# The running sum of squares of a pre-norm, added by DMA transfers in place of VectorE, in a two-layer encoder trunk

## The chip, the core and the metric

The kernel runs on one core of a Trainium2 chip. The core's engines have queues of their own and work side by side: TensorE (PE in the profile; PEld is its loading of weights), VectorE (DVE), ScalarE (ACT), GpSimd (POOL) and SyncE (SP). SP issues the transfers of the kernel before; 16 DMA engines carry them. The metric is the device time of one execution in microseconds (us), as the median of the runs.

## The reference

A streaming encoder trunk of two layers on 1024 frames of width 1024, in float32. Each layer has a mixer (layer 0: stick-breaking attention beside a multi-scale pooling; layer 1: gated linear attention) and then a gated MLP with a causal depthwise convolution of width 3. Both have an RMS norm ahead. Cut to the part around the change:

```python
def rms_norm(x, gain):
    y = x * rsqrt(mean(x * x, axis=-1) + 1e-6)
    return y * gain

def conv_ffn(h, w_up, conv_w, conv_b, w_down):
    u = h @ w_up                              # 1024 -> 2 * 2816
    conv = conv_b + sum(conv_w[j] * shifted(u, j) for j in range(3))
    a, g = split(conv, 2, axis=-1)
    return (silu(a) * g) @ w_down

for layer in range(2):
    x = x + mixer(rms_norm(x, mix_norm))
    x = x + conv_ffn(rms_norm(x, ffn_norm[layer]), ...)
```

## The kernel before

The residual stream lies transposed in SBUF: eight tiles `x[m]` of 128 partitions (channels) x 1024 (frames). A tile is 512 KB. Every float32 product is made as three matmuls of float32r halves: a value is split into a rounded part `hi` (a cast or a scaled copy by ScalarE) and the remainder `lo` (a subtraction by VectorE), and `hi*hi + hi*lo + lo*hi` is summed in PSUM. `HALVES` are the two halves of 512 frames, `T0` and `T1` in the MLP.

The RMS norm is not applied to `x` ahead of the up-projection. The products are made from `x` times the gain, and what comes out of PSUM is multiplied by `rstd_bc`, the reciprocal root of the mean square, spread over the partitions (`evacuate`, L961). The sum of squares over channels is built in two steps: each tile is squared by ScalarE (L299 for the first tile, straight into `self.acc`; L302 for the other seven, into a tile `sq`) and added to `self.acc`; then `stats` (L254) sums `acc` over the partitions by eight small matmuls with ones. From there ScalarE takes the root (L257), VectorE the reciprocal (L259) and a diagonal (L261), and `spread` (L268, L269) makes `rstd_bc`.

The entry into the up-projection is the stretch of `ffn` from L939 to L955. It goes through the tiles in `ORDER`, (0, 4, 1, 5, 2, 6, 3, 7). For each tile the last part of the mixer's output projection is added (`add_tiles`, L772), `nm.add` stores the tile to DRAM (L288, issued by SP) and makes its blocks and its square, and TensorE fills in with the first two column tiles of the up-projection for the tile two steps earlier (`first_tile`). Then come the last two of these, `nm.stats`, one more column tile (`plain`, with weights split at L796 and L797), `nm.spread`, and the evacuation.

```python
        for n, m in enumerate(ORDER):
            if n >= 2:
                add_tiles(ow, mixt, otags, [m])
            nm.add(m, x[m])
            if n >= 2:
                first_tile(n - 2)
```

`NormBlocks.block` (L282 by ScalarE, L283 by VectorE) makes the split halves of a tile, `blk`. `rsums` (L858 to L861) and `rblock` (`split`, L817 and L818) prepare sums of tiles for the products of the main loop; their tiles are `T1` to `T4`.

TensorE's order is the program's. The other engines' orders are set by a list scheduler that simulates the program while it is built. Tiles come from rotating pools: `self.acc` and the squares take slots of `xpool` (11 slots of one tile), the eight `x[m]` another eight, so there are two slots for squares; whoever takes a slot next waits until its last user is done. In the profile the sum is `nacc`, and a square is `ndg` in layer 0 and `nsq` in layer 1 (names of the slot's tile).

Of the kernel before, what the change touches and what calls it, by code (L numbers as in the profile page):

```python
# [14 lines left out]
ALU = mybir.AluOpType  # L15
# [41 lines left out]
def trunk_kernel(  # L57
# [23 lines left out]
    V, S, G, PE = nc.vector, nc.scalar, nc.gpsimd, nc.tensor  # L81
# [71 lines left out]
    class Filler:  # L153
# [3 lines left out]
        def add(self, *gens):  # L157
            self.gens += gens
# [112 lines left out]
    class NormBlocks(Norm):  # L271
# [14 lines left out]
        def add(self, m, x):  # L286
            xs[m] = dram.tile([P, T], F32, tag=f"xs{self.layer}_{m}", name="xs")
            nc.sync.dma_start(xs[m], x)  # L288
            g = pcol(self.col + m)
            if m < KT // 2:  # L290
                self.b11.append(self.block(x[:, 0:512], g))
                self.b12.append(self.block(x[:, 512:T], g))
            else:
                self.b21.append(self.block(x[:, 0:512], g))
                self.b22.append(self.block(x[:, 512:T], g))
            self.n += 1
            if self.n == 1:
                self.acc = self.acc_tile()
                S.activation(self.acc, x, AF.Square)  # L299
            else:  # L300
                sq = self.sq_tile()
                S.activation(sq, x, AF.Square)  # L302
                V.tensor_tensor(self.acc, self.acc, sq, op=ALU.add)
            if m < KT // 2:
                S.activation(x, x, AF.Copy, scale=g)

# [22 lines left out]
    def pcol(c):  # L329
        return prm[:, c:c + 1]  # L330
# [760 lines left out]
    op = ev.enter_context(tc.tile_pool(name="odd", bufs=1, reuse_waits="tile"))  # L1091
# [324 lines left out]
```

## Time and profile before

| what | before |
|---|---|
| time, median of 3 runs | 2284.07 us (2279.87 to 2284.77) |
| the profiled execution's own time | 2284.64 us |
| its span | 2282.9 us |
| TensorE busy | 2221.5 us, 97% of the span |
| VectorE busy | 1638.4 us, 72% |
| ScalarE busy | 1018.5 us, 45% |
| GpSimd busy | 360.0 us, 16% |
| DMA traffic | 178.54 MB, 78 GB/s on the mean |
| share of TensorE in the chain that ended last | 84% |

All times inside the profile are us from the start of the span. A row of a timeline gives the start, the duration, engine, line, operation, output<-input and shape, and in brackets how long the engine had been idle before it and what ended that. A row of a line gives the least, median and greatest duration in ns and the first and last start. The chain that ended last is followed back from the last instruction to what released each one. "us to landing" of a transfer runs from its issue to the arrival of its data. Layer 0's entry runs from about 430 to 493 us, layer 1's from about 1571 to 1632 us.

### The profile page before, as it was taken

How to read it: one execution, taken by the hardware profiler on the slowest of the kernel's cores; microseconds unless marked ns; L12 is line 12 of the kernel's file. 1: busy time of each engine (PE TensorE's matmuls, PEld its weight loads, DVE VectorE, ACT ScalarE, POOL GpSimd, SP SyncE). 2: the span in 40 equal slices, each digit the busy share in tenths (PEclk: the TensorE clock that was granted, in tenths of full speed). 3: DMA queues.
4: the chain of work that ended last, by engine and by line, in shares of the span. 5: the costliest groups of instructions: out<-in, count | busy, mean ns of one | idle time of the engine just before them, and what ended most of it. 6: DMA issues, size and time to landing. Idle time of an engine off the chain costs nothing.

```text
span 2282.9 us, 27335 instructions
## 1 busy us (share of the span) xinstructions
PE 2221.5 (97%) x10648; PEld 1830.4 (80%) x10648; DVE 1638.4 (72%) x2226; ACT 1018.5 (45%) x1539; POOL 360.0 (16%) x221
## 2 busy tenths in 40 slices
PE   8989989999999999999999999999999999999999
PEld 7878878877888887888887878787778888878887
DVE  5677688799999998554536555557999999985543
ACT  6667766454444444221246262527544444442210
POOL 2351330001111112421110000000011111123210
PEclk9999999999999999999999999999999999999999
DMA  4000121222222226421011011112222222264311
GB/s 143 20 30 29 48 78 53 95 84 81 83 83 83 84 83 209 160 95 53 10 39 45 21 47 38 47 38 92 84 74 83 83 84 83 83 213 147 102 47 74
DMA packets 51427, 178.54 MB, mean 78 GB/s; under 512 B 5968, under 2 KB 6608, under 8 KB 51296
## 3 DMA queue, kind: packets, MB, share of 16 engines
q1 hardware_dynamic: 51296, 176.78, 23.3%
q8 instruction: 84, 1.38, 0.2%
q14 instruction: 47, 0.39, 0.1%
HBM read 140.06 MB, written 36.70 MB: 77 GB/s over the span
## 4 chain that ended last, share of the span: by engine, by line
PE 84%; DVE 5%; ACT 4%; issue 3%; DMA 1%; POOL 1%; SPq 0%; POOLq 0%; DVEq 0%; ACTq 0%
PE lin L838 14%; PE z L838 10%; PE lin L137 6%; PE lin L139 5%; PE lin L141 5%; PE t L838 5%; PE d L838 5%; PE z L137 3%; PE z L139 3%; PE z L141 3%; PE t L137 3%; PE t L139 3%; PE t L141 3%; PE d L137 2%; PE d L139 2%
## 5 line engine op out<-in xcount | busy, mean ns | idle before, releaser
L123 ACT CAST whi<-wraw 128x1024 fp32r<-128x1024 f32 (+4 forms) x108 | 107.7, 999 | 358.2 <-PE d L139 229.8
L1030 POOL TENSOR_TENSOR c<-c 128x1024 f32<-128x1024 f32 x44 | 109.5, 2489 | 900.1 <-ACT c L1029 883.7
L864 DVE TENSOR_TENSOR u<-u,rstd_bc 128x512 f32<-128x512 f32 x160 | 159.4, 998 | 2.6
L124 DVE TENSOR_TENSOR wlo<-wraw,whi 128x1024 fp32r<-128x1024 f32 (+3 forms) x94 | 134.5, 1431 | 36.0 <-ACT whi L123 35.1
L909 ACT ACTIVATE c<-u,prm 128x1024 f32<-128x1024 f32 x88 | 109.6, 1245 | 76.6 <-DVE u L864 74.7
L1059 POOL TENSOR_TENSOR act<-a,act 128x1024 fp32r<-128x1024 f32 x40 | 105.8, 2654 | 217.3 <-ACT act L1058 210.8
L631 DVE TENSOR_TENSOR_SCAN pt<-pt,z 128x128 f32<-128x128 f32 (+3 forms) x96 | 93.2, 970 | 51.3 <-ACT z L624 50.0
L137 PE MATMUL lin<-h_hi,whi 128*128 128x512 f32 x304 | 120.1, 433 | 7.0 <-ACT whi L123 6.9
L912 DVE SCALAR_TENSOR_TENSOR c<-u,prm,c 128x1022 f32<-128x1022 f32 x88 | 120.9, 1374 | 0.1
L772 DVE TENSOR_TENSOR x<-x,t 128x512 f32<-128x512 f32 x105 | 71.8, 684 | 66.9 <-PE t L141 66.6
L910 DVE SCALAR_TENSOR_TENSOR c<-u,prm,c 128x1023 f32<-128x1023 f32 x88 | 112.5, 1279 | 7.0 <-ACT c L909 6.8
L141 PE MATMUL lin<-h_hi,wlo 128*128 128x512 f32 x304 | 110.7, 403 | 4.9 <-POOL wlo L124 4.9
L838 PE MATMUL d<-T,a 128*128 128x512 f32 x480 | 115.3, 389 | 0.0
L772 DVE TENSOR_TENSOR x<-x,d 128x512 f32<-128x512 f32 x105 | 71.8, 684 | 57.3 <-PE d L141 57.3
L139 PE MATMUL lin<-h_lo,whi 128*128 128x512 f32 x304 | 110.2, 401 | 1.1 <-DVE h_lo L240 1.1
L838 PE MATMUL z<-blk,s34h 128*128 128x512 f32 x320 | 100.6, 395 | 5.4 <-DVE u L895 5.4
L838 PEld LDWEIGHTS d<-T,a 128*128 128x128 f32 x480 | 90.1, 188 | 18.7
L817 ACT CAST s12h<-s 128x1024 fp32r<-128x1024 f32 x42 | 44.2, 1053 | 134.6 <-PE lin L838 131.2
L838 PE MATMUL lin<-T,s34h 128*128 128x512 f32 x320 | 98.9, 390 | 2.5 <-ACT tm L886 2.5
L838 PE MATMUL z<-blk,s12h 128*128 128x512 f32 x320 | 100.7, 396 | 0.0
L838 PE MATMUL lin<-blk,whi 128*128 128x512 f32 x320 | 99.9, 393 | 0.0
L838 PE MATMUL lin<-T,s12h 128*128 128x512 f32 x320 | 99.5, 392 | 0.0
(424 smaller groups left out, 6399.9 us busy)
## 6 DMA issues: line engine op xcount, KB each, us to landing
wraw<-in_wup SPq DMA_DIRECT2D x44, 512.0 KB, 3.6
act<-c SPq DMA_DIRECT2D x44, 512.0 KB, 2.6
wraw<-in_wdn SPq DMA_DIRECT2D x44, 512.0 KB, 3.7
raw_g<-in_wup SPq DMA_DIRECT2D x40, 512.0 KB, 3.6
a<-act SPq DMA_DIRECT2D x40, 512.0 KB, 4.4
xs<-x SPq DMA_DIRECT2D x16, 512.0 KB, 2.6
x<-xs SPq DMA_DIRECT2D x16, 512.0 KB, 5.4
x<-in_xT SPq DMA_DIRECT2D x8, 512.0 KB, 5.4
```

The lines of the kernel that those rows point to most:

```text
L123: S.copy(hi[:, cs], raw[:, cs])
L124: (eng or V).tensor_tensor(lo[:, cs], raw[:, cs], hi[:, cs].bitcast(F32), op=ALU.subtract)
L137: PE.matmul(out[i], wh, ah[i], start=first, stop=False)
L139: PE.matmul(out[i], wh, al[i], start=False, stop=False)
L141: PE.matmul(out[i], wl, ah[i], start=False, stop=last)
L772: V.tensor_tensor(x[m][:, cs], x[m][:, cs], pss[m][i], op=ALU.add)
L838: PE.matmul(ps, w, m, start=first and k == 0 and n == 0, stop=k == 3 and n == 2, skip_group_check=True)
L864: V.tensor_tensor(dst, dst, rstd_bc[:, cs], op=ALU.mult)
L909: S.activation(c, u, AF.Identity, scale=pcol(b + 2), bias=pcol(b + 3))
L910: V.scalar_tensor_tensor(c[:, 1:], u[:, :T - 1], pcol(b + 1), c[:, 1:], op0=ALU.mult, op1=ALU.add)
L912: V.scalar_tensor_tensor(c[:, 2:], u[:, :T - 2], pcol(b), c[:, 2:], op0=ALU.mult, op1=ALU.add)
L1030: G.tensor_tensor(ca, ca, cg, op=ALU.mult)
```

## The change

In `NormBlocks.add` the seven additions of a square to the running sum leave VectorE. In their place GpSimd issues a DMA transfer from the square to the sum, both in SBUF, which adds to what stands at its destination.

```diff
@@ class NormBlocks, def add(self, m, x) @@
             else:
                 sq = self.sq_tile()
                 S.activation(sq, x, AF.Square)
-                V.tensor_tensor(self.acc, self.acc, sq, op=ALU.add)
+                G.dma_start(self.acc, sq, accum_op=ALU.add)
             if m < KT // 2:
                 S.activation(x, x, AF.Copy, scale=g)
```

`NormBlocks` serves both layers' entries into the MLP, so 14 additions become 14 transfers. The other norm's class, `Norm`, is not touched.

What the builder made of it, in layer 0 (layer 1 reads alike). In the rows below `waits` names what an instruction waits for besides its place in the queue: an engine, `DMAHW` for a transfer that SP issues, `DMASW` with a number for a transfer that GpSimd issues (`DMASW0` is layer 0's first, `DMASW6` its seventh). GpSimd's queue from before the entry to the first pass of the main loop (L1030), with + for what is new:

```order
 L124 TENSOR_TENSOR wlo_3766<-wraw_3764,whi_3765 128x1024 [waits DMAHW0_49,PE_49,Activation_49]
+L303 DMA nacc_4488<-ndg_4499 128x1024 [waits PE_49,Activation_49]
+L303 DMA nacc_4488<-ndg_4526 128x1024 [waits DMASW0_49,Activation_49]
+L303 DMA nacc_4488<-ndg_4566 128x1024 [waits DMASW1_49,Activation_49]
+L303 DMA nacc_4488<-ndg_4605 128x1024 [waits DMASW2_49,Activation_49]
+L303 DMA nacc_4488<-ndg_4645 128x1024 [waits DMASW3_49,Activation_49]
+L303 DMA nacc_4488<-ndg_4684 128x1024 [waits DMASW4_49,Activation_49]
+L303 DMA nacc_4488<-ndg_4724 128x1024 [waits DMASW5_49,Activation_49]
 L1030 TENSOR_TENSOR c_4987<-c_4987,c_4988 128x1024 [waits Activation_49]
```

Seven transfers stand in a row, each waiting for the one before it and for ScalarE's square. ScalarE's queue at the last two squares (`ndg_4684`, `ndg_4724`), before:

```order
L302 ACTIVATE ndg_4684<-x_3952 128x1024 [waits DVE_49]
L282 ACTIVATE blk_4678<-x_3952,prm_77 128x512 [waits PE_49,Pool_49]
L796 CAST whi_4831<-wraw_4829 128x1024
L282 ACTIVATE blk_4681<-x_3952,prm_77 128x512 [waits PE_49]
L282 ACTIVATE blk_4718<-x_4372,prm_77 128x512 [waits DVE_49,PE_49]
L282 ACTIVATE blk_4721<-x_4372,prm_77 128x512 [waits DVE_49]
L302 ACTIVATE ndg_4724<-x_4372 128x1024 [waits Activation_49]
L817 CAST T4_4743<-x_4099 128x512 [waits Activation_49]
```

and now:

```order
L302 ACTIVATE ndg_4684<-x_3952 128x1024 [waits DMASW3_49,DVE_49]
L282 ACTIVATE blk_4678<-x_3952,prm_77 128x512 [waits PE_49,Pool_49]
L796 CAST whi_4831<-wraw_4829 128x1024
L282 ACTIVATE blk_4681<-x_3952,prm_77 128x512 [waits PE_49]
L282 ACTIVATE blk_4718<-x_4372,prm_77 128x512 [waits DVE_49,PE_49]
L282 ACTIVATE blk_4721<-x_4372,prm_77 128x512 [waits DVE_49]
L302 ACTIVATE ndg_4724<-x_4372 128x1024 [waits DMASW4_49,Activation_49]
L817 CAST T4_4743<-x_4099 128x512 [waits DMASW5_49,Activation_49]
```

The order is the same here; the squares have come to wait for the transfer two before their own, which read the same slot, and the first T4 tile for the sixth. VectorE's queue around the blocks of the last tiles, before:

```order
L303 TENSOR_TENSOR nacc_4488<-nacc_4488,ndg_4684 128x1024 [waits DVE_49,Activation_49]
L772 TENSOR_TENSOR x_4372<-x_4372,d_4701 128x512 [waits PE_49]
L283 SCALAR_TENSOR_TENSOR blk_4678<-x_3952,prm_77,blk_4678 128x512 [waits Activation_49]
L859 SCALAR_TENSOR_TENSOR x_3776<-x_4306,prm_77,x_3776 128x512 [waits DVE_49]
L797 TENSOR_TENSOR wlo_4832<-wraw_4829,whi_4831 128x1024 [waits DMAHW0_49,Activation_49]
L283 SCALAR_TENSOR_TENSOR blk_4681<-x_3952,prm_77,blk_4681 128x512 [waits Activation_49]
```

and now:

```order
L772 TENSOR_TENSOR x_4372<-x_4372,t_4700 128x512 [waits PE_49]
L283 SCALAR_TENSOR_TENSOR blk_4678<-x_3952,prm_77,blk_4678 128x512 [waits Activation_49]
L772 TENSOR_TENSOR x_4372<-x_4372,d_4701 128x512 [waits PE_49]
L797 TENSOR_TENSOR wlo_4832<-wraw_4829,whi_4831 128x1024 [waits DMAHW0_49,Activation_49]
L283 SCALAR_TENSOR_TENSOR blk_4681<-x_3952,prm_77,blk_4681 128x512 [waits DVE_49,Activation_49]
```

The addition is gone from ahead of the block `blk_4681`, and L859 has moved ahead of this stretch. TensorE's and SP's orders are the same as before; the first statistics matmul (L254) now waits for `DMASW6`.

## The prediction

> **What bounds the kernel now.** I read the engines' busy times first, then the chain that ended last, then the two stretches where the added lines run, engine by engine.
>
> ```profile
> PE 2221.5 (97%) x10648; PEld 1830.4 (80%) x10648; DVE 1638.4 (72%) x2226; ACT 1018.5 (45%) x1539; POOL 360.0 (16%) x221
> ...
> PE 84%; DVE 5%; ACT 4%; issue 3%; DMA 1%; POOL 1%; SPq 0%; POOLq 0%; DVEq 0%; ACTq 0%
> ```
>
> TensorE bounds the kernel: 97% busy, and 84% of the chain. VectorE counts only where TensorE waits for it. The two entries are such places on paper (columns: stretch, its length, busy us of PE, PEld, DVE, ACT and POOL, granted clock, DMA share, GB/s):
>
> ```profile
> 442.00:447.00 5.00, 5.00 (x23) 4.11 (x22) 5.00 (x7) 2.96 (x4) 0.00 (x0) 1.00 0.27 107
> 467.00:472.00 5.00, 4.51 (x20) 3.33 (x18) 5.00 (x7) 4.80 (x7) 0.00 (x0) 1.00 0.27 109
> 1576.00:1616.00 40.00, 37.63 (x162) 30.02 (x161) 39.87 (x58) 27.64 (x37) 0.00 (x0) 1.00 0.31 119
> ```
>
> VectorE is full in both entries (39.87 of 40 us in layer 1's), GpSimd is empty, and the DMA engines are about 30% used. TensorE is nearly full all the same. Its waits and the statistics matmuls, from its timeline and the chain:
>
> ```profile
> 440.71 0.50 PE L139 MATMUL lin<-blk,s12h 128*128 128x512 f32 x1 [1.22 <-DVE blk L283]
> ...
> 472.29 0.50 PE L139 MATMUL lin<-blk,s12h 128*128 128x512 f32 x1 [0.78 <-DVE blk L283]
> ...
> 477.44 1.68 PE t L254 x16
> ...
> 1611.11 0.50 PE L139 MATMUL lin<-blk,s12h 128*128 128x512 f32 x1 [0.78 <-DVE blk L283]
> ...
> 1616.26 1.68 PE t L254 x16
> ```
>
> The statistics (L254) read the finished sum. They start at 477.44 and 1616.26 with no wait ahead: the sum is early. Only the 0.78 us waits come after the first addition.
>
> **The change part by part.** *Removed: 14 additions of VectorE, 7 in each layer.*
>
> ```profile
> L303 DVE TENSOR_TENSOR nacc<-nacc,ndg x7: 1219/1224/1225, 442.5 to 474.1; 128x1024 f32<-128x1024 f32 x7
> L303 DVE TENSOR_TENSOR nacc<-nacc,nsq x7: 1211/1215/1218, 1581.3 to 1613.0; 128x1024 f32<-128x1024 f32 x7
> ```
>
> That is 14 x 1.22 = 17.1 us of VectorE's time. What of it stands on the path is seen before the wait at 472.29, in VectorE's own rows:
>
> ```profile
> 467.29 1.22 DVE L303 TENSOR_TENSOR nacc<-nacc,ndg 128x1024 f32<-128x1024 f32 x1
> 468.42 0.68 DVE L772 TENSOR_TENSOR x<-x,d 128x512 f32<-128x512 f32 x1
> 469.02 0.75 DVE L283 SCALAR_TENSOR_TENSOR blk<-x,prm,blk 128x512 fp32r<-128x512 f32 x1
> 469.68 0.75 DVE L859 SCALAR_TENSOR_TENSOR x<-x,prm 128x512 f32<-128x512 f32 x1
> 470.35 1.22 DVE L797 TENSOR_TENSOR wlo<-wraw,whi 128x1024 fp32r<-128x1024 f32 x1
> 471.48 2.08 DVE L283 SCALAR_TENSOR_TENSOR blk<-x,prm,blk 128x512 fp32r<-128x512 f32 x3
> ```
>
> From 467.29 to 471.48 VectorE has no gap, so the addition (1.13 us to the next start) and L859, which now stands well ahead of this stretch (0.67 us), leave the block up to 1.8 us earlier. TensorE waits 0.78 us for it, so 0.78 us is the gain, once in each layer: -1.6 us. The wait at 440.71 is ahead of the first addition (442.5) and stays. The other additions are hidden by TensorE's matmuls already: nothing.
>
> *Added: 7 transfers in a row.* Each waits on GpSimd's queue for its square and for the transfer before it, since both write the same sum. ScalarE has two buffers for squares, so from the third on a square waits for the transfer two before it, and blocks of later tiles stand behind that square on ScalarE. What else stands behind: on GpSimd only L1030, which starts at 507.3 (row below); on ScalarE the cast of T4 waits for the sixth transfer, ahead of a weight cast; on VectorE T4's remainder does so too; on TensorE the statistics wait for the seventh, and everything after them queues behind. SP's own order is unchanged; its 8 stores of x share the DMA engines. Let L be the time from a square's end, or from the previous transfer's landing, to a transfer's landing. The squares:
>
> ```profile
> L302 ACT ACTIVATE ndg<-x x7: 1040/1044/1065, 439.3 to 470.6; 128x1024 f32<-128x1024 f32 x7
> L302 ACT ACTIVATE nsq<-x x7: 1041/1044/1062, 1578.9 to 1609.4; 128x1024 f32<-128x1024 f32 x7
> ...
> 456.15 1.04 ACT L302 ACTIVATE ndg<-x 128x1024 f32<-128x1024 f32 x1
> ...
> 1594.99 1.04 ACT L302 ACTIVATE nsq<-x 128x1024 f32<-128x1024 f32 x1
> ...
> 507.30 3.39 POOL L1030 TENSOR_TENSOR c<-c 128x1024 f32<-128x1024 f32 x1 [157.90 <-ACT c L1029]
> ```
>
> The seventh transfer lands no earlier than 440.3 + 7L (all in a row after the first square), 457.2 + 4L (after the fourth) and 471.7 + L (after the last); in layer 1 that is 1579.9 + 7L, 1596.0 + 4L and 1610.4 + L. TensorE, 0.78 us sooner, asks for it at 476.66 and 1615.48. So it is hidden while L is under 4.86 us: (476.66 - 457.2)/4, and (1615.48 - 1596.0)/4.
>
> *What is L?* No row shows an accumulating transfer, nor one that GpSimd issues. The nearest:
>
> ```profile
> act<-c SPq DMA_DIRECT2D x44, 512.0 KB, 2.6
> ...
> a<-act SPq DMA_DIRECT2D x40, 512.0 KB, 4.4
> xs<-x SPq DMA_DIRECT2D x16, 512.0 KB, 2.6
> ...
> out_yT<-x SPq DMA_DIRECT2D x16, 256.0 KB, 2.0
> ```
>
> A transfer of the same tile out of SBUF lands in 2.6 us (xs, act), half of it in 2.0: 1.2 us for the data and 1.4 us fixed. An accumulation must read the sum as well as the square; if both reads pass one after the other, the data cost 2.4 us: 3.8 us. GpSimd's issuing is unknown: its bounds are nothing, and one of its own passes over such a tile:
>
> ```profile
> L1030 POOL TENSOR_TENSOR c<-c 128x1024 f32<-128x1024 f32 x44 | 109.5, 2489 | 900.1 <-ACT c L1029 883.7 <-DVE c L912 16.4
> ```
>
> So L lies between 2.6 us (a plain transfer) and 3.8 + 2.5 = 6.3 us; the farthest composition is a load and a store end to end, 4.4 + 2.6 = 7.0 us. I take 4.7 us, 3.8 and some 0.9 for the issuing, as 128 rows of addresses should cost less than a pass over 128x1024 elements; this is an estimate. Then the seventh lands by 476.4 and 1615.1, under 0.6 us ahead of TensorE, and the sixth near 471.3, when ScalarE reaches T4's cast:
>
> ```profile
> 471.57 1.12 ACT L817 CAST T<-x 128x512 fp32r<-128x512 f32 x2
> ```
>
> So the transfers cost nothing; their cover is the 36 us of matmuls that TensorE has anyway. If L passes 4.86 us, the statistics are late next.
>
> [...]
>
> **The sum**, against the profiled execution's own 2284.64 us (span 2282.9 and 1.7 around it): 2284.64 - 2 x 0.78 = 2283.1 us. That execution is 0.6 us above the median of the runs, 2284.07, so against the median it would read 2282.5. A measurement of this kernel tells 0.2%, 4.6 us, from no change; this is no change.
>
> **The rivals.**
>
> *The chain of transfers binds (slower).* Place: the wait of L254. It decides from L = 4.86 us on; then each further us of L costs 4 to 7 us a layer. For: seven links, each with the full latency, a margin of 0.2 us of L, and the stores of x and weight loads on the same DMA engines. At 5.5 us the sum lands at 479.2 and 1618.0, 1.75 + 1.77 us late: 2288.2. From there TensorE's clock falls too:
>
> ```profile
> 149.36 0.79 PE L141 MATMUL lin<-h_hi,wlo 128*128 128x512 f32 x1 [4.86 <-POOL wlo L124]
> ...
> 149.00:155.00 6.00, 5.64 (x19) 4.77 (x20) 3.56 (x6) 2.04 (x5) 5.05 (x8) 0.50 0.30 87
> 155.00:160.00 5.00, 4.64 (x30) 3.89 (x29) 2.75 (x5) 3.51 (x7) 3.27 (x5) 0.99 0.26 104
> ...
> 1154.15 0.39 PE L1147 MATMUL t<-whi,h_hi 128*128 128x272 f32 x1 [1.10 <-ACT whi L123]
> 1155.48 0.59 PE L1148 MATMUL t<-wlo,h_hi 128*128 128x272 f32 x1 [0.94 <-DVE wlo L124]
> ...
> 1157.00:1165.00 8.00, 8.00 (x38) 8.00 (x38) 1.82 (x3) 1.01 (x3) 0.00 (x0) 0.50 0.15 57
> ```
>
> After a wait of 4.86 us the clock stands at 0.50 for 6 us, which is 3.0 us of work lost; after two waits of 2.04 us together, for 8 us and more. At L = 6.3 us the sum lands at 440.3 + 44.1 = 484.4 and 1624.0: 7.0 + 7.8 late, and 6.0 for the clock: 2305.4. At 7.0 us: 11.9 + 12.7 + 6.0, 2315. Against: it needs over 1 us beyond the data and the fixed share that the stores show.
>
> [...]
>
> *The freed VectorE pays more (faster).* It could also shorten the first wait of each entry (1.22 at 440.71, 1.59 below) and the one after the statistics:
>
> ```profile
> 1579.55 0.50 PE L139 MATMUL lin<-blk,s12h 128*128 128x512 f32 x1 [1.59 <-DVE blk L283]
> ...
> 490.77 1.23 DVE L797 TENSOR_TENSOR wlo<-wraw,whi 128x1024 fp32r<-128x1024 f32 x1 [0.33 <-ACT whi L796]
> ...
> 492.65 0.50 PE L137 MATMUL lin<-blk,whi 128*128 128x512 f32 x1 [0.82 <-DVE u L961]
> ```
>
> With all of it, the last taken twice: 2283.1 - 1.2 - 1.6 - 1.6 = 2278.7. Against: VectorE is idle for 0.33 us ahead of that weight row already, so it carries no backlog there, and the first wait of an entry is ahead of the change.
>
> **How the numbers follow.** L under 4.86 us, the forecast: 0.45, 2283.1. L of 4.86 to 5.5 us, up to 2288: 0.13, nearly all within 0.2%. L above that, 2289 to 2315: 0.38. VectorE pays more: 0.04. So faster 0.04, same 0.56, slower 0.40. The forecast's own range is 2280 to 2286. The whole range goes down to 2279 (all waits gone) and up to 2308, L near 6.5 us (8.4 + 9.2 + 6.0 = 23.6 us), which leaves about 0.18 above.
>
> **What would show it.** Right: 14 rows of L303 under GpSimd, landing in under 4.9 us each; L254 at its old distance from the matmuls ahead of it; no 0.78 us wait for L283; VectorE some 17 us less busy. Wrong: L254 waiting for the sum, squares of ScalarE waiting for transfers, a clock of 0.50 in the stretch behind, all of which come from L alone. A wait elsewhere would mean that I misread the order.

## The result: 12 us slower, and the profile after

| what | before | after |
|---|---|---|
| time, median of 6 runs each, on one chip | 2284.42 us (2279.87 to 2285.66) | 2296.53 us (2294.06 to 2301.88) |
| the profiled execution's own time, its span | 2284.64, 2282.9 us | 2296.37, 2294.6 us |
| ratio to before | | 1.0062, 95% interval 1.0047 to 1.0077 |

The change makes the kernel slower by 0.6%. From the page of the changed kernel: the engines' busy times, the chain that ended last, the queue of the transfers that GpSimd issues (packets, MB, share of 16 engines' span), and the groups of DMA issues (KB each, median us to landing).

```profile
PE 2225.0 (97%) x10648; PEld 1833.9 (80%) x10648; DVE 1623.9 (71%) x2212; ACT 1017.8 (44%) x1539; POOL 372.4 (16%) x235
...
q0 software_dynamic: 2016, 7.34, 1.7%
...
PE 83%; DVE 5%; ACT 5%; issue 3%; DMA 2%; POOL 1%; SPq 0%; POOLq 0%; DVEq 0%; ACTq 0%
...
nacc<-ndg POOLq DMA_DIRECT2D x7, 512.0 KB, 5.1
nacc<-nsq POOLq DMA_DIRECT2D x7, 512.0 KB, 5.2
```

VectorE is 14.5 us less busy without its 14 additions, and 14 transfers of 512 KB have come, with a landing 5.1 to 5.2 us after the issue. The chain shows what they do: DMA goes from 1% to 2% of the span and VectorE stays at 5%, so the time that VectorE gave up was hardly on the path. GpSimd's timeline through layer 0's entry shows the seven transfers in a row; behind it, from the view of line L303, their least, median and greatest landing:

```profile
438.18 1.04 POOL L303 DMA_DIRECT2D nacc<-ndg  x1 [91.27 <-ACT ndg L302]
444.99 0.86 POOL L303 DMA_DIRECT2D nacc<-ndg  x1 [5.77 <-ACT x L305]
450.49 0.85 POOL L303 DMA_DIRECT2D nacc<-ndg  x1 [4.64 <-ACT blk L282]
456.14 0.85 POOL L303 DMA_DIRECT2D nacc<-ndg  x1 [4.80 <-ACT blk L282]
461.23 0.85 POOL L303 DMA_DIRECT2D nacc<-ndg  x1 [4.24 <-DMA nacc<-ndg]
468.36 0.86 POOL L303 DMA_DIRECT2D nacc<-ndg  x1 [6.28 <-ACT blk L282]
474.79 0.85 POOL L303 DMA_DIRECT2D nacc<-ndg  x1 [5.56 <-DMA nacc<-ndg]
```

```profile
DMA to landing us min/median/max: 4.5/5.2/6.8
```

The issues stand 5.1 to 7.1 us apart, and from the second on each square was ready 3 to 6 us before its issue (the last one starts at 468.1, and no square waits for a transfer). The releasers named on ScalarE, as `blk L282`, are put down by time: such a block ends near the landing that the queue waits for. The first square ends at 437.86, so the seven links take (479.37 - 437.86)/7 = 5.93 us each, up to TensorE's first statistics matmul; in layer 1 it is (1623.68 - 1583.25)/7 = 5.78. TensorE's timeline has what that costs; below it, for comparison, the statistics of layer 0 and the wait for `u` in layer 1 in the kernel before:

```profile
438.23 0.50 PE L139 MATMUL lin<-blk,s12h 128*128 128x512 f32 x1 [1.22 <-DVE blk L283]
...
479.37 3.57 PE L254 MATMUL t<-ones,nacc 128*128 128x2 f32 x16 [5.45 <-DMA nacc<-ndg]
...
497.95 0.50 PE L137 MATMUL lin<-blk,whi 128*128 128x512 f32 x1 [0.82 <-DVE u L961]
...
1582.86 0.50 PE L139 MATMUL lin<-blk,s12h 128*128 128x512 f32 x1 [1.60 <-DVE blk L283]
1623.68 3.58 PE L254 MATMUL t<-ones,nacc 128*128 128x2 f32 x16 [5.14 <-DMA nacc<-nsq]
...
1643.47 0.50 PE L137 MATMUL lin<-blk,whi 128*128 128x512 f32 x1 [0.82 <-DVE u L961]
```

```profile
477.27 1.84 PE L254 MATMUL t<-ones,nacc 128*128 128x2 f32 x16
...
1631.53 0.49 PE L137 MATMUL lin<-blk,whi 128*128 128x512 f32 x1 [0.82 <-DVE u L961]
```

The statistics, which waited for nothing before, wait 5.45 and 5.14 us for the last transfer, and then run at half speed (3.57 us in place of 1.84). The 0.78 us wait for L283 is gone in both layers; the first wait of each entry is as it was. Stretches of the changed kernel, with the columns as before (granted clock third from the end, then DMA share and GB/s):

```profile
438.00:480.00 42.00, 36.31 (x156) 29.32 (x157) 33.48 (x52) 25.51 (x35) 6.17 (x7) 0.99 0.70 177
479.40:486.00 6.60, 6.60 (x24) 5.92 (x25) 5.58 (x10) 3.72 (x5) 0.00 (x0) 0.51 0.36 90
1623.70:1633.00 9.30, 9.30 (x30) 8.04 (x31) 8.32 (x13) 4.77 (x6) 0.00 (x0) 0.51 0.39 115
```

Behind the wait the clock stands at 0.51, for 6.6 and 9.3 us: 6.6 x 0.49 = 3.2 and 9.3 x 0.49 = 4.6 us of work lost. In the entry itself the DMA engines are now 70% busy.

The length of an entry, from TensorE's first wait to its wait for `u` (L961), closes the account. Layer 0: 51.94 us before (440.71 to 492.65), 59.72 after (438.23 to 497.95), +7.78. Up to the wait of L254 it is 0.87 us faster than before, the wait is 5.45, and the rest, 3.20, is the slow clock's. Layer 1: 51.98 before, 60.61 after, +8.63 = -0.87 + 5.14 + 4.36. Together the two entries are 16.4 us longer. The profiled executions differ by 11.7 us in their spans and the medians by 12.1: the 4.7 us between 16.4 and 11.7 lie outside the entries. Such stretches vary between executions: in the profiled runs of this document layer 0's first wait, up to which their source is the same, stands anywhere from 438.2 to 442.0 us.

### The profile page after: what moved, and what is told of

Its sections match the earlier page's. It is cut to its first block, busy times and chain, and to the rows that moved or that the text cites. A ratio compares the mean times of both kernels' runs of the same rounds, so it can differ in the third digit from the quotient of the medians.

```text
span 2294.6 us, 27371 instructions
## 1 busy us (share of the span) xinstructions
PE 2225.0 (97%) x10648; PEld 1833.9 (80%) x10648; DVE 1623.9 (71%) x2212; ACT 1017.8 (44%) x1539; POOL 372.4 (16%) x235
## 4 chain that ended last, share of the span: by engine, by line
PE 83%; DVE 5%; ACT 5%; issue 3%; DMA 2%; POOL 1%; SPq 0%; POOLq 0%; DVEq 0%; ACTq 0%
PE lin L838 14%; PE z L838 10%; PE lin L137 5%; PE lin L139 5%; PE lin L141 5%; PE t L838 5%; PE d L838 5%; PE z L137 3%; PE z L139 3%; PE z L141 3%; PE t L137 3%; PE t L139 3%; PE t L141 3%; PE d L137 2%; PE d L139 2%
## 5 line engine op out<-in xcount | busy, mean ns | idle before, releaser
L1030 POOL TENSOR_TENSOR c<-c 128x1024 f32<-128x1024 f32 x44 | 109.3, 2484 | 735.1 <-ACT c L1029 718.4
```

What stands on the lines that cost most here:

```text
L1030: G.tensor_tensor(ca, ca, cg, op=ALU.mult)
```

## The experiments

Two theories were open. A: a link's own time is about 5 us, and the stores of x on the same DMA engines add the rest. A rival: a link takes so long by itself, with or without stores. And one question on L's parts: is it GpSimd's issuing, or the addition in the transfer, that makes it so long?

**The changed kernel without the stores of x.**

```diff
-            xs[m] = dram.tile([P, T], F32, tag=f"xs{self.layer}_{m}", name="xs")
-            nc.sync.dma_start(xs[m], x)
...
-            nc.sync.dma_start(x[m], xs[m])
+            nc.sync.dma_start(x[m], xT[m * P:(m + 1) * P, :])
```

> The changed kernel without the eight stores of x that each entry makes to DRAM; the residual that is loaded back later is read from the kernel's input instead, so that part of the output is left out. Theory A (the seven transfers run one behind the other, and each is lengthened by the stores and weight loads that share the DMA engines): a link, from one transfer's start to the next one's, falls from 5.9 us on the mean (41.5 us from the first square's end to the statistics, over 7) towards the undisturbed 4.5 to 4.7 us; the wait of the statistics falls from 5.45 and 5.14 us to under 1 us each, and the time falls by 9 to 14 us against the changed kernel, to 2283 to 2288 us. Rival B (an accumulating transfer takes 5 to 7 us by itself, whatever else runs): links of 5.5 us and more, waits of 4 us and more, time within 4 us of the changed kernel's 2296.5.

It took 2280.35 us, ratio to before 0.9986 (0.9977 to 0.9995), some 3 us under the range that was expected. The fourth, fifth and seventh issue in GpSimd's timeline:

```profile
454.94 0.85 POOL L301 DMA_DIRECT2D nacc<-ndg  x1 [4.21 <-DMA nacc<-ndg]
460.01 0.85 POOL L301 DMA_DIRECT2D nacc<-ndg  x1 [4.21 <-DMA nacc<-ndg]
...
470.85 0.85 POOL L301 DMA_DIRECT2D nacc<-ndg  x1 [4.96 <-ACT ndg L300]
```

The landing, from the view of the transfers' line:

```profile
DMA to landing us min/median/max: 4.5/4.5/4.8
```

TensorE's statistics in both layers, and a stretch behind each of them:

```profile
475.68 1.95 PE L254 MATMUL t<-ones,nacc 128*128 128x2 f32 x16 [0.37 <-DMA nacc<-ndg]
...
1610.76 1.95 PE L254 MATMUL t<-ones,nacc 128*128 128x2 f32 x16 [0.39 <-DMA nacc<-nsq]
```

```profile
478.20:481.50 3.30, 3.30 (x9) 2.54 (x9) 3.30 (x7) 2.05 (x4) 0.00 (x0) 0.50 0.17 17
...
1612.00:1617.00 5.00, 5.00 (x27) 4.24 (x27) 4.99 (x9) 3.32 (x5) 0.00 (x0) 1.00 0.35 107
```

With eight stores fewer in each entry the links become regular: 5.06 us from issue to issue, a landing of 4.5 and 0.56 us from there to the next issue. The statistics wait 0.37 and 0.39 us. So 5.06 us is the link's own time, and 0.7 to 0.9 us of the 5.8 to 5.9 come from the stores. By the prediction's border of 4.86 us, four links of 5.06 us behind the fourth square should make the statistics 0.8 us late; they were 0.4 us late, and not for that reason. The seventh issue, at 470.85, waits for the last square and not for the transfer before it. With the additions gone from VectorE the fourth square comes 2.8 us earlier: in the changed kernel, whose row is below, it starts 12.65 us behind the entry's first wait (438.23), in the kernel before 15.44 us (456.15 and 440.71). So it binds nothing.

```profile
450.88 1.05 ACT L302 ACTIVATE ndg<-x 128x1024 f32<-128x1024 f32 x1
```

What is left is the whole chain and the last square with one link behind it. Without the stores the chain would be done 0.7 us early: the first square ends at 439.23 (the prediction's 440.3, with an entry that starts 1.1 us sooner), seven links of 5.06 end at 474.65, and TensorE asks at 475.31. It is the last square, with its one link, that makes the statistics 0.37 us late. With the stores the chain binds: at 5.93 us a link it is 6.1 us longer, which is the 0.7 us that it had to spare and the 5.45 us of waiting.

**The kernel before without the stores of x**, as the control: the same lines left out, the additions on VectorE.

> The kernel before with the same part left out (no stores of x in the entries, the residual read from the input), to read the run above by. Both theories: within 3 us of the kernel before, 2281 to 2287 us, since SP's stores are not waited for there.

2282.97 us, ratio 1.0000 (0.9989 to 1.0011). The stores by themselves cost nothing that the measurement can tell; it is only beside the transfers that they matter.

**Four transfers, then three additions on VectorE.**

```diff
-                G.dma_start(self.acc, sq, accum_op=ALU.add)
+                if self.n <= 5:
+                    G.dma_start(self.acc, sq, accum_op=ALU.add)
+                else:
+                    V.tensor_tensor(self.acc, self.acc, sq, op=ALU.add)
```

> The first four additions of each layer as transfers, the last three on VectorE again. Theory A (only the end of the chain costs): the fourth transfer lands about 461 us, some 8 us ahead of the last square, no wait of the statistics, clock 0.99 and more, 2283 to 2286 us. Rival C (transfers that GpSimd issues cost time wherever they stand, or the new order of the instructions does): four sevenths of the loss remain, 2290 to 2293 us.

2287.88 us, ratio 1.0018 (1.0008 to 1.0029): a little over what was expected. No wait of L254, but another one, first on VectorE and then on TensorE:

```profile
462.69 1.23 DVE L306 TENSOR_TENSOR nacc<-nacc,ndg 128x1024 f32<-128x1024 f32 x1 [2.94 <-DMA nacc<-ndg]
...
472.48 0.50 PE L139 MATMUL lin<-blk,s12h 128*128 128x512 f32 x1 [1.54 <-DVE blk L283]
```

The first of VectorE's three additions waits 2.94 us for the fourth transfer. VectorE starts nothing in these 2.94 us, and what is queued behind the addition comes later, the block of 472.48 too: TensorE waits 1.54 us (1.90 in layer 1) where it waited 0.78. The chain that is cut short is late here at the place where it is joined.

**All seven additions by GpSimd's own arithmetic**, without a transfer.

```diff
-                G.dma_start(self.acc, sq, accum_op=ALU.add)
+                G.tensor_tensor(self.acc, self.acc, sq, op=ALU.add)
```

> All seven additions of each layer by GpSimd's own elementwise pass (2.5 us each in the rows of the other norm) instead of a transfer: VectorE is freed just as in the changed kernel, the order of the instructions is of the same kind, and the link is 2.5 to 3.2 us. Theory A: the last one ends some 3 us behind the last square, before TensorE asks; no wait of the statistics; 2282 to 2285 us, of which up to 1.6 us below the kernel before shows the freed VectorE. Rival C (the new order costs): 2288 us and more.

2296.68 us, ratio 1.0058 (1.0046 to 1.0071), against an expectation of no change. GpSimd's third pass, a VectorE instruction beside it, and TensorE:

```profile
453.19 3.32 POOL L303 TENSOR_TENSOR nacc<-nacc,ndg 128x1024 f32<-128x1024 f32 x1 [5.82 <-ACT ndg L302]
...
454.17 2.90 DVE L859 SCALAR_TENSOR_TENSOR x<-x,prm 128x512 f32<-128x512 f32 x1
...
474.52 0.50 PE L137 MATMUL lin<-blk,s12h 128*128 128x512 f32 x1 [2.27 <-ACT blk L282]
```

VectorE's 32 block instructions here, and then in the kernel with the transfers:

```profile
L283 DVE SCALAR_TENSOR_TENSOR blk<-x,prm,blk x32: 737/742/2903, 434.3 to 1622.6; 128x512 fp32r<-128x512 f32 x32
```

```profile
L283 DVE SCALAR_TENSOR_TENSOR blk<-x,prm,blk x32: 741/745/752, 431.5 to 1613.8; 128x512 fp32r<-128x512 f32 x32
```

The pass ends at 456.51 and the VectorE instruction that started at 454.17 ends 0.56 us later: 2.90 us for one that takes 0.74 elsewhere. A block instruction takes up to 2.90 us too; beside transfers, none takes over 0.752. Each of layer 0's seven GpSimd passes has one such stretch beside it and holds up VectorE by 1.5 to 2.2 us, more than the 1.22 us that the addition took there. VectorE falls behind, blocks come late, and TensorE waits 2.27 us and, behind that, 1.06 and 1.60 us more; its clock is 0.63 on the mean from 475 to 480 us and 0.69 from 480 to 485. The statistics wait for nothing, as expected: what failed is the price that VectorE pays.

**Half the data, no addition, and SyncE as issuer.** Three kernels price the parts of L. The first adds only half the columns, the second copies the square onto the sum without adding, the third does that from SyncE's queue. Each has one of the three new lines (the comments are added here).

```diff
-                G.dma_start(self.acc, sq, accum_op=ALU.add)
+                G.dma_start(self.acc[:, 0:512], sq[:, 0:512], accum_op=ALU.add)   # half
+                G.dma_start(self.acc, sq)                                         # copy
+                nc.sync.dma_start(self.acc, sq)                                   # copy, SyncE
```

> The transfers of the changed kernel, but each adds only the first 512 of the 1024 columns (256 KB in place of 512 KB); the squares of the other columns are left out of the sum. Theory A (the link's time is the transfer's own, made of GpSimd's issuing 0.85 us, a fixed part and the data, and the stores of x lengthen it): the profile of the changed kernel has 2.79 us of DMA engine time for 512 KB, so half the data take 1.4 us off: an undisturbed link of 5.06 - 1.4 = 3.7 us, at most 4.5 beside the stores, under the 4.86 at which the chain binds. No wait of L254 over 0.4 us, no fall of the clock, 2281 to 2285 us. Theory C (the link is mostly fixed: issuing, semaphores and the hand-over between queues, whatever the size): link over 4.9 us, L254 waits 2 us or more in each layer, 2288 to 2295 us.

> The transfers of the changed kernel, in the same places and of the same size, but as plain copies of the square onto the sum, without adding; the sum is left out. Theory A (the addition costs the second read: engine time 2.79 us in place of 1.56 us for 512 KB): an undisturbed link of 5.06 - 1.2 = 3.8 us, up to 4.6 beside the stores, under 4.86; no wait of L254 over 0.4 us, 2281 to 2285 us. Theory C (adding costs nothing, the size and the issuing by GpSimd make the link): link 5.1 to 5.9 us as with the addition, L254 waits about 5 us in each layer, 2294 to 2299 us.

> As the plain copies of the square onto the sum, without adding, but issued by SyncE in place of GpSimd, in SyncE's own queue among the loads of weights and the stores of x; the sum is left out. It prices GpSimd's issuing: Theory A, landing 2.6 to 3.0 us after the issue as the stores of x do, and a link shorter by about the 0.85 us that GpSimd spends on an issue. Theory C (GpSimd's part is the smaller one): link within 0.4 us of the copy that GpSimd issues. No statement on the time: SyncE's queue waits for the squares and the loads behind them may come late.

The half took 2280.26 us, ratio 0.9989 (0.9979 to 0.9999), the copy 2280.59 us, 0.9990 (0.9980 to 1.0000), SyncE's copy 2280.32 us in its one run; the first two are just under the 2281 to 2285 us that were expected. No L254 waits in any of them. Issues and landing, from the view of the transfers' line: of the half, of GpSimd's copy, of SyncE's copy; last, from the page of GpSimd's copy, the queue of its transfers:

```profile
L303 POOL DMA_DIRECT2D nacc<-ndg x7: 852/854/1042, 441.9 to 473.3; - x7
DMA to landing us min/median/max: 3.2/3.4/4.6
```

```profile
L303 POOL DMA_DIRECT2D nacc<-ndg x7: 530/530/746, 438.8 to 470.1; - x7
DMA to landing us min/median/max: 2.8/2.9/4.9
```

```profile
L303 SPq DMA_DIRECT2D nacc<-nsq x7: 470/471/471, 1576.7 to 1607.2; - x7
DMA to landing us min/median/max: 2.9/3.0/4.8
```

```profile
q0 software_dynamic: 2016, 7.34, 0.8%
```

GpSimd's copy lands as soon as SyncE's (2.8 and 2.9 us at the least): who issues makes no difference that these rows can show. The addition does: 4.5 against 2.8 us for the same 512 KB. Its engine time is 1.7% of 2294.6 us over 14 transfers, 2.79 us each, against 0.8% of 2278.5 us, 1.30 us, for the copy: the factor of two that two reads would give (a count of the reads themselves is in no trace). The instruction that issues it is longer too, 0.85 against 0.53 us. Half the data take 4.5 - 3.2 = 1.3 us off the landing, about half the engine time. The links of the copies, which their expectations spoke of, can't be read off: in GpSimd's copy almost every issue waits for its square and not for the copy before it.

**One transfer alone**: the sixth addition, that ahead of the block for which TensorE waited 0.78 us.

```diff
-                G.dma_start(self.acc, sq, accum_op=ALU.add)
+                if self.n == 7:
+                    G.dma_start(self.acc, sq, accum_op=ALU.add)
+                else:
+                    V.tensor_tensor(self.acc, self.acc, sq, op=ALU.add)
```

> Only the sixth of the seven additions of each layer is a transfer, that which stands on VectorE ahead of the block for which TensorE waits 0.78 us; the other six stay on VectorE. Theory A: the transfer is issued after the fifth addition, near 466 and 1604 us, and lands 4.5 to 6 us later, by 472 and 1610, before VectorE comes to the seventh addition near 474 and 1613. No chain, no wait of L254; the 0.78 us waits go: 1.6 us less than before, 2281 to 2284 us, a ratio of 0.998 to 1.0005 to before. Rival: the seventh addition waits for the transfer in VectorE's queue, as with four transfers, and what stands behind it makes TensorE late: 2285 to 2289 us.

2285.37 us, ratio 1.0006 (0.9995 to 1.0017): not to be told from before. The rival's wait on VectorE did not come, but the other half of the expectation was wrong as well. TensorE in both layers, and VectorE ahead of the first of the two blocks:

```profile
472.37 0.50 PE L139 MATMUL lin<-blk,s12h 128*128 128x512 f32 x1 [0.41 <-DVE blk L283]
...
1611.13 0.50 PE L139 MATMUL lin<-blk,s12h 128*128 128x512 f32 x1 [0.42 <-DVE blk L283]
```

```profile
467.13 0.69 DVE L775 TENSOR_TENSOR x<-x,t 128x512 f32<-128x512 f32 x1 [0.15 <-PE t L141]
468.50 0.69 DVE L775 TENSOR_TENSOR x<-x,d 128x512 f32<-128x512 f32 x1 [0.68 <-PE d L141]
...
469.77 0.74 DVE L862 SCALAR_TENSOR_TENSOR x<-x,prm 128x512 f32<-128x512 f32 x1
470.44 1.22 DVE L800 TENSOR_TENSOR wlo<-wraw,whi 128x1024 fp32r<-128x1024 f32 x1
471.57 1.41 DVE L283 SCALAR_TENSOR_TENSOR blk<-x,prm,blk 128x512 fp32r<-128x512 f32 x2
```

0.37 and 0.36 of the 0.78 us are gone, not all of it. The addition's 1.13 us came free, but VectorE now waits 0.15 and 0.68 us of it for TensorE's products `t` and `d`; and L859 (L862 here) still stands ahead of the block, which in the changed kernel it doesn't. So the part of the gain that the prediction gave to L859's move (0.67 us) would have covered what is left; no run has that move alone. The entries are 51.58 and 51.64 us long, 0.36 and 0.34 less than before.

**Two half transfers for each addition**: the whole computation, as two chains.

```diff
-                G.dma_start(self.acc, sq, accum_op=ALU.add)
+                for cs in HALVES:
+                    G.dma_start(self.acc[:, cs], sq[:, cs], accum_op=ALU.add)
```

> The whole computation, with each of the 14 transfers cut into two of 512 columns: two chains that need not wait for each other, issued one behind the other by GpSimd. Theory A (a link is the hand-over, the issue, a fixed part and the data in series, and only what is in series counts): each half's link is 3.9 us undisturbed as in the run with half the columns, some 4.6 beside its partner and the stores, under 4.86; the sum is ready ahead of L254, the 0.78 us waits are gone: 2280 to 2284 us, a ratio to before of 0.998 to 1.000. Rival (the two halves share the DMA engines and GpSimd's issuing of twice 0.85 us, so that a step takes as long as one whole transfer or longer): a step of 5.0 to 6.0 us, L254 waits 1 to 6 us in each layer, 2286 to 2300 us.

2279.30 us, ratio 0.9993 (0.9982 to 1.0004). Its issues and landing, and TensorE's rows:

```profile
L304 POOL DMA_DIRECT2D nacc<-ndg x14: 850/859/1212, 438.8 to 470.7; - x14
DMA to landing us min/median/max: 3.3/4.3/5.8
```

```profile
474.45 1.90 PE L254 MATMUL t<-ones,nacc 128*128 128x2 f32 x16
489.92 0.50 PE L137 MATMUL lin<-blk,whi 128*128 128x512 f32 x1 [0.82 <-DVE u L962]
...
1608.78 1.91 PE L254 MATMUL t<-ones,nacc 128*128 128x2 f32 x16
1624.25 0.50 PE L137 MATMUL lin<-blk,whi 128*128 128x512 f32 x1 [0.82 <-DVE u L962]
```

The same data are added by the same engines, with the stores in place, and the statistics wait for nothing. The issues of one half stand 3.8 to 5.6 us apart through the first five additions, some of them held by a square, where some 4.6 were expected. It is not that the DMA engines have less to do: in layer 1's entry they are 87% busy from 1574 to 1610 us, against 73% in the changed kernel from 1583 to 1624. What the rows suggest is that one half moves while the other lands and is handed over. The entries are 51.02 us (from 438.90) and 50.99 us (from 1573.26) long, 0.92 and 0.99 less than before. Against the changed kernel that is the whole loss back (its interval, 1.0047 to 1.0077, lies clear of this one, each taken against the kernel before on the same chip); against the kernel before, the 1.9 us are less than the measurement can tell. No kernel here is shown to be faster than before with the whole computation in it.

## Why the prediction was wrong

The forecast was no change, 2283.1 us; what came was the first rival, the chain that binds. By steps:

- **What bounds, and what the removed additions were worth: right.** The 0.78 us waits went and nothing else did: 0.87 us an entry with the queueing around them. The second rival, a freed VectorE that pays more, did not happen: the first waits (1.22, 1.60) and that for `u` (0.82) stand in the trace as before.
- **The failed step is "What is L?": the sum has no term for the stores of x on the same DMA engines.** It took 4.7 us; the links took 5.93 and 5.78, and 5.06 without the stores. The prediction named the sharing (the stores, the weight loads) as a word for the rival and put it at nothing: the rows had the engines at 27 to 31% busy, which was read as room. But the transfers bring 7 x 2.8 us into 36 us, and with both the engines are 70% busy; a link is 0.7 to 0.9 us longer. Seven times that is 5 to 6 us a layer, which is nearly the whole wait: without the stores it was 0.37 and 0.39 us, and the time 2280.35.
- **The undisturbed link was too short by 0.36 us as well, 4.7 in place of 5.06, which alone cost next to nothing.** The terms, with what they measured: data 2.4 us, measured 2.8 of engine time; fixed 1.4, measured 4.5 - 2.8 = 1.7, in which lies the instruction that issues (0.85 us for an addition, 0.53 for a copy). The 0.9 us on top for GpSimd's issuing was the author's estimate, and no run shows such a term: GpSimd's copy lands as early as SyncE's, 2.8 and 2.9 us behind the issue at the least. What was left out instead is the 0.56 us from a landing to the next issue, which no transfer that stands alone shows.
- **The formula held, the border did not.** With the measured links the row for all seven gives 440.3 + 7 x 5.93 - 476.66 = 5.15 us late in layer 0 and 1579.9 + 7 x 5.78 - 1615.48 = 4.88 in layer 1; the waits were 5.45 and 5.14. The 0.3 us between are the start of L254, 477.27 in the timeline where the prediction used 477.44, and the 0.09 us by which TensorE was sooner than its 0.78. The clock's 3.0 us a layer were 3.20 and 4.36. The sum, 2283.1 + 5.15 + 4.88 + 6.0 = 2299.1, is 14.5 us above the profiled 2284.64, where the entries are 16.4 us longer; that it lies only 2.8 us over the profiled 2296.4 is in part luck, since 4.7 us went elsewhere. The border of 4.86 came from the fourth square where it stood before the change; with VectorE freed that square is 2.8 us earlier, and the rows give (473.92 - 437.86)/7 = 5.15 us for the chain. Among the signs of being wrong, one did not come: no square waits for a transfer. On ScalarE it is T4's cast that waits, 5.16 us, and TensorE does not wait for that.
- **The estimate of the added reads held** in that an addition takes the DMA engines twice as long as a copy, 2.79 against 1.30 us for 512 KB.
- The prediction's bounds for L, 2.6 to 6.3 us, held what came, and so did its range for the time. Within them no row told 4.7 us from 5.9, and the forecast took the side of the border that costs nothing.

Shown is: the stores' share (without them the wait is all but gone, and the control does not move), the addition's share (the copy lands 1.7 us sooner), and that it is the serial chain that costs (the same bytes in two chains cost nothing). Argued, not shown: that it is the time of the DMA engines which stores and transfers share, and not something else on their way; which of the stores meets which link; and what part the weight loads have in it, which were left in place in all runs. Why 0.56 us pass from a landing to the next issue stays open.

## What to carry to other kernels

Price a chain of dependent transfers by its link, from landing to landing. Here that was 1.7 us for issue and fixed part, 2.8 us for the data of an addition (1.3 for a copy), 0.56 us to the next issue, and 0.7 to 0.9 us more beside the stores of x, all of it times seven. A margin of 0.2 us on a link that comes seven times was none, and DMA engines that had been 27 to 31% busy were 70% busy with the chain, whose own transfers take 7 x 2.8 of 36 us. When such a chain is late, cut it into chains that don't depend on each other, before anything is moved back: here two halves hid what one whole could not. Take the times of what feeds the chain with the change in place: here the fourth square came 2.8 us earlier once VectorE was freed. And count for work that is taken off a busy engine only the waits that stand behind it, here 0.8 us of 8.5 a layer.

## What the runs showed of the hardware

- Beside each of layer 0's seven GpSimd passes over 128x1024 (2.36 to 3.32 us each) VectorE's work took 1.5 to 2.2 us longer than the same instructions elsewhere; the addition itself had taken VectorE 1.22 us. A single SCALAR_TENSOR_TENSOR of 128x512 took up to 2.90 us in place of 0.74.
- A transfer that adds took the DMA engines 2.79 us for 512 KB, a copy 1.30; GpSimd's instruction that issues it 0.85 us against 0.53. From its landing to the next dependent issue 0.56 us passed (5.06 - 4.5).
- With a wait of 0.37 us ahead of the small statistics matmuls the clock stood at 0.50 for 3.3 us in layer 0, and after 0.39 us in layer 1 it stayed at 1.00, as it did behind these matmuls in both layers of the kernel before, where they wait for nothing. Why one of two like waits has a slow stretch behind it, no run here shows.
